# Handing out the side work of a two-layer hybrid encoder by its estimated ScalarE and VectorE time instead of by fixed rates

## The chip, the cores and the metric

The kernel runs on one core of one Trainium2 chip. The metric is the device time of one execution in microseconds, as a median of several runs; the profile shows one execution, with a span from its first to its last instruction.

## The reference

The input is a sequence of 512 tokens of 1024 channels in float32. Two layers run one after the other, each with three residual blocks behind an RMSNorm:

```
h = h + 1/2 * SwiGLU_1(RMSNorm(h))        # 1024 -> 2816 -> 1024
h = h + Mixer(RMSNorm(h))
h = h + 1/2 * SwiGLU_2(RMSNorm(h))
```

The mixer has one input projection of 7168 columns that feeds three branches, and all of them are projected, gated by sigmoids of the input, summed and projected once more:

- a Hyena branch: two long convolutions of 512 channels over time, with gates between them, whose filters come from a small sine network (in the kernel: transforms by matmul, called "filter" for the spectra of the filters and "hyena" for the convolutions);
- dilated sliding-window attention in three groups of eight heads, with a position bias (in the kernel: "bias" writes rows of the bias to DRAM, "attn0" and "attn1" each do four heads of all three groups);
- a gated linear recurrence forward and backward over time (in the kernel "rg").

After the second layer comes a last RMSNorm.

## The kernel before

Every large projection is computed with weights and activations split into two parts of reduced mantissa (float32r), as three matmuls: hi by hi, lo by hi, hi by lo. The work is a list, `prog`, of **main steps**. A step loads a block of weights (`load`, L220: 512 rows by 256 columns, 512 KB, two buffers `raw`), splits it (`prep`: a copy on ScalarE into `whi`, L238, and a subtraction on VectorE into `wlo`, L239; twice 128x512 a step, five buffers each), and then issues 24 matmuls of 512 columns (`pair` and `mm3`, L166 to L168). `load` and `prep` run up to three steps ahead. Two such steps make a pair of outputs, which is evacuated from PSUM by `evac` on ScalarE and VectorE; the pool for these outputs has three buffers.

The **side work** (filter, bias, vecs, rg, hyena, attn and some small ones) is written as generators: each piece up to a `yield` is one side step, with its own small matmuls, ScalarE and VectorE instructions and DMAs. `push` puts a generator on one of two lanes, `pump(n)` runs n side steps and takes turns between the lanes, and `drain(name)` runs the rest of a generator at once, because what follows in the list needs its result (or its buffers). The program is traced in this order, and each engine works through its instructions in an order that the scheduler of the framework makes from it: earlier in the trace goes first where both are ready.

The rate decides how many side steps follow a main step:

```
                credit[0] += rate[0]
                pump(int(credit[0]))
                credit[0] -= int(credit[0])
```

The rate is 1 in general, RF = 1.35 from the push of "filter" to its drain, and RM = 1.6 from the push of "rg" to the end of the mixer. These rates count steps, whatever is in them.

Main steps of a mixer, numbered from 1, as the prediction uses them: 1 to 8 the input of rg (after which `push("rg")` follows); 9 to 26 `quad(0)`, the values, queries and keys of four heads (25 and 26 the last keys, evacuated by `together`, L1221), then `push("attn0")`; 27 to 30, 31 to 34 and 35 to 38 the three inputs of Hyena (`conv_in`; after the first of them `push("hyena")`); 39 to 50 `gateproj(2)`, four times two steps of gate (tile `gt`) and one of projection (tile `pj`), with `drain("rg")` after step 40; then `drain("attn0")`; 51 to 68 `quad(1)`, then `push("attn1")`; 69 to 80 `gateproj(0)` with `drain("hyena")` after step 70, since the projection of step 71 reads what Hyena made; 81 to 92 `gateproj(1)` with `drain("attn1")` after step 82; 93 to 100 the output projection.

One half of one order of "hyena" (there are four of them) has these side steps: two transposes with a split (zt), two transforms (xf: twelve matmuls of 256 columns each, L790 to L793 behind them), one of six VectorE operations (zm, zp; L799 to L804), two of four (L809 to L815), one of six (ua to wb; L819 to L826), an empty one, and two that transform back (yc: eight matmuls, then L841, L842, and in the second order the split into yah and yal that `pj` reads). The first of "bias" are three empty steps, and then 24 that each copy one small tile (`row`, L574) and write it 16 times to DRAM (L575).

Of the kernel before, what the change touches and what calls it, by code (L numbers as in the profile page):

```python
# [19 lines left out]
F32R = mybir.dt.float32r  # L20
# [11 lines left out]
NS = 35  # L32
HP = 20
F0, F1 = 0, 6
RF, RM = 1.35, 1.6
TWO_PI = 2.0 * math.pi


def shape_constants():
# [65 lines left out]
    ("hy_skip", 8), ("rg_conv_w", 16), ("rg_conv_b", 4),  # L105
    ("rg_ba", 8), ("rg_bx", 8), ("rg_lambda", 8), ("b_gate", 24),
]


@with_exitstack  # L110
def trunk(ctx: ExitStack, tc: tile.TileContext, A, out, depth=DEPTH):
    nc = tc.nc
# [17 lines left out]
    def slot(name, dt=F32):  # L130
        return sp.tile([128, 2, 512], dt, tag="sl", name=name)

    def tmp(name, dt=F32):
        return tp.tile([128, 512], dt, tag="t", name=name)
# [10 lines left out]
    def flat(t):  # L145
        return t.rearrange("p a b -> p (a b)")

    def split(hi, lo, src):
        S.copy(hi, src)
        V.tensor_tensor(lo, src, hi.bitcast(F32), ALU.subtract)  # L150
# [28 lines left out]
    def main(fn, src=None, kc=4, cols=256):  # L179
        prog.append((fn, src, kc, cols, 0))  # L180

    def pump(n, lane=None):
        for _ in range(n):
            live = [q for q in lanes if q]
            if lane is not None:
                live = [q for q in live if q is lane]
            while live:
                q = live[turn[0] % len(live)]
                turn[0] += 1
                try:  # L190
                    next(q[0][1])
                    break
                except StopIteration:
                    alive.discard(q[0][0])
                    q.popleft()
                    live = [x for x in live if x]
            else:
                return

    def push(name, gen, lane=0):  # L200
        alive.add(name)
        lanes[lane].append((name, gen))

    def drain(name):
        while name in alive:
            pump(1, next(q for q in lanes if any(n == name for n, _ in q)))

    rate, credit = [1], [0]
    first = [True]

    def run_prog():
        wsteps = [i for i, p in enumerate(prog) if p[1] is not None]
        raws, made = {}, {}
        nxt_raw, nxt_prep = [0], [0]

        def load(j):
            _, src, kc, cols, _ = prog[wsteps[j]]
            raw = rp.tile([128, 4, 256], F32, tag="raw", name="raw")
            if cols == 256:
                nc.sync.dma_start(raw[:, :kc], src.rearrange("(k p) n -> p k n", p=128))  # L220
            else:
                for k in range(kc):
                    dst, rows = raw[:, 2 * k:2 * k + 2], slice(128 * k, 128 * k + 128)
                    nc.sync.dma_start(dst, src[rows].rearrange("p (g c) -> p g c", c=256)
                                      if len(src.shape) == 2 else src[rows])
            raws[j] = raw

        def prep(j, half=None):
            _, src, kc, cols, _ = prog[wsteps[j]]
            if cols == 512:  # L230
                kc *= 2
            raw = raws[j]
            parts = made.setdefault(j, [])
            for k0 in range(0, kc, 2) if half is None else (2 * half,):
                kk = min(2, kc - k0)
                hi = wp.tile([128, 2, 256], F32R, tag="hi", name="whi")
                lo = wp.tile([128, 2, 256], F32R, tag="lo", name="wlo")
                S.copy(hi[:, :kk], raw[:, k0:k0 + kk])  # L238
                V.tensor_tensor(lo[:, :kk], raw[:, k0:k0 + kk], hi.bitcast(F32)[:, :kk], ALU.subtract)  # L239
                if cols == 512:  # L240
                    parts.append((flat(hi), flat(lo)))
                    continue
                for k in range(kk):
                    parts.append((hi[:, k], lo[:, k]))
            if half in (None, 1):
                del raws[j]

        def ahead(n):
            while nxt_raw[0] < min(n, len(wsteps)):
                load(nxt_raw[0])  # L250
                nxt_raw[0] += 1

        def prepare(n):
            while nxt_prep[0] < min(n, len(wsteps)):
                prep(nxt_prep[0])
                nxt_prep[0] += 1

        norm = state["norm"]
        load_x(0)
        ahead(1)  # L260
        load_x(1)
        norm.squares(0)
        norm.half(0, lambda i: i in (1, 2) and prep(0, i - 1))
        nxt_prep[0] = 1
        ahead(2)
        norm.copies()
        norm.half(1)
        prepare(2)
        norm.copies()
        norm.squares(1)  # L270
        norm.end()
        j = 0
        for i, (fn, src, kc, cols, _) in enumerate(prog):
            if src is None:
                fn()
            else:
                with tc.high_priority(HP):
                    ahead(j + 3)
                    prepare(j + 3)
                fn(made.pop(j))  # L280
                j += 1
                credit[0] += rate[0]
                pump(int(credit[0]))
                credit[0] -= int(credit[0])
        pump(10 ** 6)

    def pair(W, X, evac, name):
# [151 lines left out]
    def h(k):  # L439
        return hs[k // 2][:, k % 2]  # L440
# [9 lines left out]
    def load_x(a):  # L450
        if a == 0:
            rows_to_cols(g0, A["ffn1_norm"][0], 8)
        for b in range(4):
            nc.sync.dma_start(xt[b][:, a], A["x"][b::4, a * 512:a * 512 + 512])
# [41 lines left out]
    hyst = [dict() for _ in range(depth)]  # L496

    def ffn(l, which, next_norm):
        wg, wu, wd = A[f"ffn{which}_wg"][l], A[f"ffn{which}_wu"][l], A[f"ffn{which}_wd"][l]
        hid = []  # L500
        X = lambda: state["norm"].x
        for fp in range(DFF // 256):
            st = {}

            def ev_g(c, ps, st=st):
                t = tmp("silu")
                V.tensor_tensor(t, ps, state["norm"].R, ALU.mult)  # L507
                S.activation(t, t, AF.Silu)
                st[c] = t

            def ev_u(c, ps, st=st):
                if c == 0:
                    st["hi"], st["lo"] = slot("hidh", F32R), slot("hidl", F32R)
                t = tmp("up")
                V.tensor_tensor(t, ps, state["norm"].R, ALU.mult)  # L515
                V.tensor_tensor(t, t, st[c], ALU.mult)
                split(st["hi"][:, c], st["lo"][:, c], t)
                hid.append((st["hi"][:, c], st["lo"][:, c]))

            pair(wg[:, fp * 256:(fp + 1) * 256], X, ev_g, "g")  # L520
            pair(wu[:, fp * 256:(fp + 1) * 256], X, ev_u, "u")
            if which == 1 and fp == F0:
                main(lambda: (push("filter", hy_filter(l, hyst[l])), rate.__setitem__(0, RF)))
            if which == 1 and fp == F1:
                main(lambda: (drain("filter"), rate.__setitem__(0, 1)))
                if l == 0:
                    main(lambda: (push("bias", bias_rows()), push("vecs", load_vectors(range(1, depth), 4))))

        def begin():
            state["next"] = next_norm()  # L530

        if next_norm is None:
            down_tokens(wd, hid)
            return
        main(begin)
        for d in range(4):
            def ev_d(c, ps, d=d):
                k = 2 * d + c
                V.scalar_tensor_tensor(h(k), ps, 0.5, h(k), ALU.mult, ALU.add)
                state["next"].add(k, h(k))  # L540

            pair(wd[:, d * 256:(d + 1) * 256], lambda: hid, ev_d, "d")

        def end():
            hid.clear()
            state["next"].end()
            state["norm"] = state["next"]

        main(end)
# [589 lines left out]
    def mixer(l, next_norm):  # L1139
# [50 lines left out]
                pair(W[:, c0 + o + i * 256:c0 + o + i * 256 + 256], X, ev, key)  # L1190
        main(lambda: drain("xn"))
        main(lambda: push("rg", rg(l, srg)))
        main(lambda: rate.__setitem__(0, RM))

        def apart(st, g, c, ps):

# [162 lines left out]
        def end():  # L1359
            state["next"].end()  # L1360
            state["norm"] = state["next"]
            del state["mx"]
            rate[0] = 1

        main(end)


# [81 lines left out]
    for l in range(depth):  # L1449
# [6 lines left out]
        else:  # L1456
            main(lambda: push("ht", to_tokens()))
            ffn(l, 2, None)
    run_prog()


# [33 lines left out]
```

## Time and profile before

| | us |
|---|---|
| median of three runs | 2874.32 |
| lowest and highest of them | 2872.74, 2874.44 |
| the profiled execution | 2872.54 |
| its span | 2870.8 |
| TensorE busy in the span | 2838.4 |
| VectorE busy | 1693.0 |
| ScalarE busy | 1220.3 |
| mean granted clock of TensorE | 0.996 |

The profiled execution lasts 1.74 us longer than its span and 1.78 us less than the median of the runs. Matmuls overlap in the records, so that a busy TensorE can still run below its full pace; the number of matmuls in a stretch shows that better than the busy time.

### The profile page before, as it was taken

The page shows a single profiled execution, that of the slowest core. Times are in us where ns is not written, and L with a number is a line of the kernel's source. Part 1 is how long each engine was busy: PE and PEld are TensorE (multiplying, and loading weights), DVE is VectorE, ACT ScalarE, POOL GpSimd, SP SyncE. Part 2 cuts the span into 40 slices and gives each one's busy share as a digit, 9 for nine tenths or more (in the row PEclk, how much of TensorE's full clock was granted, in tenths as well). Part 3 has the DMA queues.
Part 4 walks back from the last instruction along what each step waited for, and adds up shares of the span by engine and source line. Part 5 has one row for each costly group of instructions (what it writes and reads, how often), then busy time and mean ns, then how long its engine had stood idle before and what let it go on. Part 6 is the DMA issues. An engine that isn't in the chain of part 4 may idle for free.

```text
span 2870.8 us, 35848 instructions
## 1 busy us (share of the span) xinstructions
PE 2838.4 (99%) x13379; PEld 2360.9 (82%) x13379; DVE 1693.0 (59%) x3076; ACT 1220.3 (43%) x2133; POOL 172.5 (6%) x321
## 2 busy tenths in 40 slices
PE   9999999999999999999999999999999999999998
PEld 7887888778888888888888888887888888888887
DVE  5784447586776555444377743566757755654533
ACT  5442335845333543333244432377443353433323
POOL 2011110010001000000010000001100110000000
PEclk9999999999999999999999999999999999999999
DMA  4436633242233233332334333333322322333332
GB/s 139 129 112 130 137 118 103 83 121 94 81 96 92 67 125 96 98 101 93 99 110 137 114 96 114 114 98 102 106 88 88 101 80 74 125 96 96 96 103 96
DMA packets 260735, 297.54 MB, mean 104 GB/s; under 512 B 14196, under 2 KB 241632, under 8 KB 260560
## 3 DMA queue, kind: packets, MB, share of 16 engines
q1 hardware_dynamic: 244240, 256.41, 29.1%
q0 software_dynamic: 16160, 38.77, 5.6%
q8 instruction: 105, 1.72, 0.2%
q14 instruction: 70, 0.57, 0.1%
q10 hardware_dynamic: 160, 0.07, 0.0%
HBM read 276.84 MB, written 18.35 MB: 103 GB/s over the span
## 4 chain that ended last, share of the span: by engine, by line
PE 91%; ACT 4%; DVE 2%; DMA 1%; issue 1%; ACTq 0%; DVEq 0%
PE g L166 6%; PE g L167 6%; PE g L168 6%; PE u L166 5%; PE u L167 5%; PE u L168 5%; PE d L168 4%; PE d L167 4%; PE d L166 4%; PE gt L166 3%; PE gt L168 3%; PE gt L167 3%; PE pj L167 1%; PE pj L168 1%; PE pj L166 1%; PE y L1435 1%
## 5 line engine op out<-in xcount | busy, mean ns | idle before, releaser
L239 DVE TENSOR_TENSOR wlo<-raw,whi 128x512 fp32r<-128x512 f32 x928 | 635.9, 689 | 784.8 <-ACT whi L238 773.1
L238 ACT CAST whi<-raw 128x512 fp32r<-128x512 f32 x928 | 572.8, 620 | 1074.6 <-PE u L167 232.1
L166 PE MATMUL g<-xh,whi 128*128 128x512 f32 x696 | 273.3, 393 | 2.8 <-DVE up L515 2.8
L166 PE MATMUL u<-xh,whi 128*128 128x512 f32 x704 | 275.2, 391 | 0.0
L167 PE MATMUL u<-xl,whi 128*128 128x512 f32 x704 | 274.7, 390 | 0.0
L168 PE MATMUL u<-xh,wlo 128*128 128x512 f32 x704 | 274.6, 390 | 0.0
L167 PE MATMUL g<-xl,whi 128*128 128x512 f32 x696 | 272.2, 391 | 0.0
L168 PE MATMUL g<-xh,wlo 128*128 128x512 f32 x696 | 272.2, 391 | 0.0
L166 PE MATMUL d<-hidh,whi 128*128 128x512 f32 x528 | 205.9, 390 | 0.0
L168 PE MATMUL d<-hidh,wlo 128*128 128x512 f32 x528 | 205.8, 390 | 0.0
L167 PE MATMUL d<-hidl,whi 128*128 128x512 f32 x528 | 205.7, 390 | 0.0
L166 PEld LDWEIGHTS g<-xh,whi 128*128 128x128 f32 x696 | 131.3, 189 | 30.7 <-DVE up L515 3.9
L168 PEld LDWEIGHTS u<-xh,wlo 128*128 128x128 f32 x704 | 132.3, 188 | 27.3
L166 PEld LDWEIGHTS u<-xh,whi 128*128 128x128 f32 x704 | 132.3, 188 | 27.2 <-DVE silu L507 0.5
L167 PEld LDWEIGHTS u<-xl,whi 128*128 128x128 f32 x704 | 132.4, 188 | 26.6
L168 PEld LDWEIGHTS g<-xh,wlo 128*128 128x128 f32 x696 | 131.2, 188 | 26.9
L167 PEld LDWEIGHTS g<-xl,whi 128*128 128x128 f32 x696 | 131.3, 189 | 26.5
L166 PE MATMUL gt<-nh,whi 128*128 128x512 f32 x384 | 152.8, 398 | 0.3 <-DVE mrg L1292 0.3
L167 PE MATMUL gt<-nl,whi 128*128 128x512 f32 x384 | 150.0, 391 | 0.0
L168 PE MATMUL gt<-nh,wlo 128*128 128x512 f32 x384 | 150.0, 391 | 0.0
L167 PEld LDWEIGHTS d<-hidl,whi 128*128 128x128 f32 x528 | 99.2, 188 | 20.6
L166 PEld LDWEIGHTS d<-hidh,whi 128*128 128x128 f32 x528 | 99.2, 188 | 20.5
(467 smaller groups left out, 5579.3 us busy)
## 6 DMA issues: line engine op xcount, KB each, us to landing
raw<-in_w_in SPq DMA_DIRECT2D x96, 512.0 KB, 3.5
raw<-in_ffn_wg SPq DMA_DIRECT2D x88, 512.0 KB, 3.7
raw<-in_ffn_wu SPq DMA_DIRECT2D x88, 512.0 KB, 3.8
raw<-in_ffn_wd SPq DMA_DIRECT2D x60, 512.0 KB, 3.5
raw<-in_w_gate SPq DMA_DIRECT2D x48, 512.0 KB, 3.6
raw<-in_ffn_wd SPq DMA_DIRECT2D x56, 256.0 KB, 2.7
raw<-in_w_in SPq DMA_DIRECT2D x32, 256.0 KB, 3.0
raw<-in_w_out SPq DMA_DIRECT2D x16, 512.0 KB, 3.4
```

What stands on the lines that cost most here:

```text
L166: T.matmul(ps, lh, rh, start=first, stop=False)
L167: T.matmul(ps, lh, rl, start=False, stop=False)
L168: T.matmul(ps, ll, rh, start=False, stop=last)
L238: S.copy(hi[:, :kk], raw[:, k0:k0 + kk])
L239: V.tensor_tensor(lo[:, :kk], raw[:, k0:k0 + kk], hi.bitcast(F32)[:, :kk], ALU.subtract)
L1435: T.matmul(ps, xh[:, tok], wh, start=(k == 0), stop=False)
```

## The change

The two rates go. After each main step `pace` sums, by a formula for each instruction that was traced since the last look, the time that ScalarE, VectorE and TensorE would take (`estimate`): 0.2 us and 0.85 ns an element of the free dimension for ScalarE, 0.15 us and 1.05 ns for VectorE (6.5 ns for a reciprocal), 0.013 us and 0.417 ns a column for a float32r matmul, and 1.7 ns a column for another. What ScalarE or VectorE have over TensorE is kept as `owed`, never below zero. Then up to LANE = 2 side steps run, and none is begun while the larger of the two debts, with the side steps just taken, is above AHEAD = 3.0 us. Drains stay as they were, and what they issue is counted at the next look. The computation is the same, instruction for instruction; what changes is where in the trace the side steps stand. The matmuls of the undilated scores (`score0`) take rounded float32r parts in both kernels: the diff doesn't touch them.

```diff
--- before.py
+++ after.py
@@ -32,7 +32,7 @@
 NS = 35
 HP = 20
 F0, F1 = 0, 6
-RF, RM = 1.35, 1.6
+AHEAD, LANE = 3.0, 2
 TWO_PI = 2.0 * math.pi
 
 
@@ -107,6 +107,20 @@
 ]
 
 
+def estimate(i):
+
+    if not i.outs:
+        return None, 0.0
+    n = math.prod(c for _, c in i.outs[0].ap[1:])
+    if i.engine == mybir.EngineType.Activation:
+        return 0, 0.2 + 0.85e-3 * n
+    if i.engine == mybir.EngineType.DVE:
+        return 1, {"InstReciprocal": 6.5e-3, "InstTensorTensorScan": 2.4e-3}.get(type(i).__name__, 1.05e-3) * n + 0.15
+    if i.engine == mybir.EngineType.PE:
+        return 2, 0.013 + 0.417e-3 * n if i.ins[1].dtype == F32R else 1.7e-3 * n
+    return None, 0.0
+
+
 @with_exitstack
 def trunk(ctx: ExitStack, tc: tile.TileContext, A, out, depth=DEPTH):
     nc = tc.nc
@@ -205,7 +219,27 @@
         while name in alive:
             pump(1, next(q for q in lanes if any(n == name for n, _ in q)))
 
-    rate, credit = [1], [0]
+    owed, given, seen = [0.0, 0.0], [0.0, 0.0, 0.0], [0]
+
+    def count():
+        todo = nc.cur_bb.bb.instructions
+        for i in todo[seen[0]:]:
+            e, t = estimate(i)
+            if e is not None:
+                given[e] += t
+        seen[0] = len(todo)
+
+    def pace():
+
+        count()
+        for e in range(2):
+            owed[e] = max(owed[e] + given[e] - given[2], 0.0)
+        given[:] = 0.0, 0.0, 0.0
+        for _ in range(LANE):
+            if max(owed[e] + given[e] for e in range(2)) > AHEAD:
+                break
+            pump(1)
+            count()
     first = [True]
 
     def run_prog():
@@ -279,9 +313,7 @@
                     prepare(j + 3)
                 fn(made.pop(j))
                 j += 1
-                credit[0] += rate[0]
-                pump(int(credit[0]))
-                credit[0] -= int(credit[0])
+                pace()
         pump(10 ** 6)
 
     def pair(W, X, evac, name):
@@ -520,9 +552,9 @@
             pair(wg[:, fp * 256:(fp + 1) * 256], X, ev_g, "g")
             pair(wu[:, fp * 256:(fp + 1) * 256], X, ev_u, "u")
             if which == 1 and fp == F0:
-                main(lambda: (push("filter", hy_filter(l, hyst[l])), rate.__setitem__(0, RF)))
+                main(lambda: push("filter", hy_filter(l, hyst[l])))
             if which == 1 and fp == F1:
-                main(lambda: (drain("filter"), rate.__setitem__(0, 1)))
+                main(lambda: drain("filter"))
                 if l == 0:
                     main(lambda: (push("bias", bias_rows()), push("vecs", load_vectors(range(1, depth), 4))))
 
@@ -1190,7 +1222,6 @@
                 pair(W[:, c0 + o + i * 256:c0 + o + i * 256 + 256], X, ev, key)
         main(lambda: drain("xn"))
         main(lambda: push("rg", rg(l, srg)))
-        main(lambda: rate.__setitem__(0, RM))
 
         def apart(st, g, c, ps):
 
@@ -1360,7 +1391,6 @@
             state["next"].end()
             state["norm"] = state["next"]
             del state["mx"]
-            rate[0] = 1
 
         main(end)
```

## Rows read from the trace of the kernel before

**Rows 1.** The page: span, then busy us, share, instructions of each engine.

```profile
span 2870.8 us, 35848 instructions
PE 2838.4 (99%) x13379; PEld 2360.9 (82%) x13379; DVE 1693.0 (59%) x3076; ACT 1220.3 (43%) x2133; POOL 172.5 (6%) x321
```

**Rows 2.** Who TensorE waited for: us in total, times, longest.

```profile
PE v L166 <- ACT k L1221: 11.3, 2, 5.9
PE g L166 <- DVE up L515: 2.8, 1, 2.8
```

**Rows 3.** Windows in SwiGLU: busy us (instructions) by engine, clock, DMA share, GB/s.

```profile
1296.00:1368.00 72.00, 72.00 (x320) 59.65 (x319) 30.08 (x45) 22.41 (x37) 0.00 (x0) 1.00 0.29 94
```

**Rows 4.** Windows, around the three stalls and around the end of attn1.

```profile
570.00:582.00 12.00, 6.64 (x23) 5.00 (x21) 11.62 (x14) 7.32 (x11) 3.69 (x7) 0.73 0.27 71
1986.00:2004.00 18.00, 12.11 (x43) 9.49 (x42) 16.32 (x21) 10.20 (x13) 4.71 (x9) 0.81 0.21 53
270.00:282.00 12.00, 9.23 (x34) 6.81 (x33) 8.43 (x16) 4.14 (x7) 1.78 (x3) 0.86 0.55 59
966.00:990.00 24.00, 23.06 (x134) 19.67 (x134) 15.60 (x16) 8.47 (x14) 0.00 (x0) 1.00 0.10 29
...
576.00:582.00 6.00, 3.58 (x9) 2.83 (x9) 5.62 (x7) 3.46 (x5) 2.59 (x5) 0.50 0.23 55
```

**Rows 5.** Groups of ScalarE, 540 to 580 us: busy us, mean ns, idle before.

```profile
L943 ACT ACTIVATE ti<-psg,vec 64x512 f32<-64x512 f32 x8 | 5.5, 683 | 0.2
...
L238 ACT CAST whi<-raw 128x512 fp32r<-128x512 f32 x9 | 5.4, 609 | 1.4 <-DMA raw<-in_w_in 1.3
L944 ACT ACTIVATE aa<-tr,rgs 128x512 f32<-128x512 f32 x4 | 3.3, 816 | 0.1
...
L946 ACT ACTIVATE qq<-aa 128x512 f32<-128x512 f32 x4 | 2.5, 618 | 0.0
```

**Rows 6.** Timeline of ScalarE ahead of the first long stall: start, us, instruction, idle.

```profile
541.25 1.28 ACT L942 ACT_TABLE_LOAD   x1
542.55 0.68 ACT L942 ACTIVATE tr<-psg,vec 64x512 f32<-64x512 f32 x1
...
575.75 2.13 ACT L149 CAST ych<-gx 128x512 fp32r<-128x512 f32 x2 [2.08 <-DVE gx L967]
577.78 1.06 ACT L1221 COPY k<-k 128x512 f32<-128x512 f32 x2
```

**Rows 7.** DMA queues, 222 to 276 us: packets, MB, share of 16 engines' stretch.

```profile
q0 software_dynamic: 869, 1.48, 38.6%
q1 hardware_dynamic: 4939, 4.89, 27.4%
...
dbias<-row POOLq DMA_DIRECT2D x8, 192.0 KB, 8.8
```

**Rows 8.** Who ScalarE waited for, 222 to 276 us.

```profile
ACT whi L238 <- DMA raw<-in_ffn_wu: 14.2, 3, 6.3
```

**Rows 9.** Tiles xf, yc, pj near 870 us: durations ns, first to last start.

```profile
L168 PE MATMUL xf<-zh,ftl x8: 279/282/284, 842.5 to 850.6; 128*128 128x256 f32 x8
...
L836 PE MATMUL yc<-invt,wa x8: 271/274/276, 872.6 to 880.8; 128*128 128x128 f32 x8
...
L166 PE MATMUL pj<-yah,whi x8: 388/390/477, 881.5 to 886.5; 128*128 128x512 f32 x8
```

**Rows 10.** Groups of VectorE, 849 to 885 us: busy us, mean ns, idle before.

```profile
L239 DVE TENSOR_TENSOR wlo<-raw,whi 128x512 fp32r<-128x512 f32 x12 | 8.2, 689 | 6.3 <-ACT whi L238 6.3
...
L819 DVE TENSOR_TENSOR ua<-yy 128x1024 f32<-128x1024 f32 x1 | 1.2, 1227 | 0.0
...
L824 DVE TENSOR_TENSOR wa<-ua 128x512 f32<-128x512 f32 x1 | 0.7, 687 | 0.0
...
L802 DVE TENSOR_TENSOR zp<-x,x 128x256 f32<-128x256 f32 x1 | 0.4, 420 | 0.0
```

**Rows 11.** Groups of TensorE, 966 to 992 us.

```profile
L166 PE MATMUL gt<-nh,whi 128*128 128x512 f32 x13 | 5.1, 390 | 0.0
```

## The prediction

> **What bounds the kernel now.** I read the page first: TensorE is busy for 2838.4 of 2870.8 us, VectorE and ScalarE for 1693.0 and 1220.3 [rows 1]. Where nothing disturbs it TensorE does 320 matmuls in 72 us, 0.225 us each [rows 3], so a main step of 24 lasts 5.4 us. The change issues no instruction less or more; it can only move the stretches in which TensorE falls behind that pace. The list of what TensorE waited for names two of weight: 11.3 us, in two pieces, before the first matmul of a pair v, for a copy k of ScalarE, and 2.8 us for VectorE's `up` [rows 2]. The windows around them show the whole loss, since the clock drops as well [rows 4]. From 570 to 582 us there are 23 matmuls where 53 fit: 30 x 0.225 = 6.8 us lost, with a granted clock of 0.50 in the second half (the lower of its two levels, 1.2 of 2.4 GHz). From 1986 to 2004 there are 43 for 80: 8.3 us. From 270 to 282 there are 34 for 53: 4.3 us. Together 19.4 us, 0.7%: this is what better spreading could win at most, but for small change.
>
> **Why those stalls are there.** The first two lie at main step 27 of each mixer, behind the densest part of rg. One gate step of rg has four tanh of 0.68, two of 0.81 and one of 0.62 on ScalarE, 5.0 us, and a main step beside it 2 x 0.61 of splits and some 0.6 to 1.2 of evacuation (an estimate: two or four instructions a pair like L238's) [rows 5]; it has 4 matmuls of its own, so TensorE needs 5.4 + 0.9 = 6.3 us while ScalarE needs 6.8 to 7.4. At a rate of 1.6, every second or third main step takes two. A table load of 1.28 us comes on top, and just before the stall two casts `ych` stand ahead of the copies of k in ScalarE's order, which wait 2.1 us for VectorE [rows 6]. The third is a different thing: the bias rows. From 222 to 276 us eight row writes of 192 KB take 38.6% of the 16 DMA engines, the weights 27.4% [rows 7], and ScalarE waits three times, 14.2 us in all, for weights to land [rows 8].
>
> **The new order, walked through the code.** The formula prices a main step at 24 x 0.2265 = 5.44 us of TensorE, and its two splits at 1.27 (ScalarE) and 1.38 (VectorE). I added the evacuation of each pair and the price of each side step by the same formula and went through the mixer step by step, from step 9 on, where the debt is nought. The results are positions, not times. (1) rg: a gate step is priced at 4.45 us of ScalarE, so they go one to a main step, at 17 to 20 and 23 to 25 and 27, with none at 26, where before two stood at 16 and at 23. rg ends at main step 35 instead of 29, before its drain at 40. (2) hyena starts at 37 instead of 32, never gets more than two steps, and is stopped whenever one of its VectorE steps (3.1 to 5.2 us by the formula) leaves more than 3.0 of debt. Its last pair xf stands behind step 69 instead of 65. At the drain behind step 70 six filled steps are left, 17.0 us of VectorE; before, none were. (3) That lump leaves 15 us of debt, so attn1 gets nothing for four main steps, and its drain behind step 82 holds 11 filled steps (14.7 ScalarE, 15.9 VectorE, 19.6 TensorE) instead of 6 (7.6, 8.3, 10.9). attn0's drain grows from 5 to 8. (4) filter: 6 instead of 12 steps are left at its drain in the first layer. (5) bias: its steps cost the formula next to nothing, so they go two to a main step: 27 in 15 main steps instead of in 27. A VectorE price 5% lower would leave hyena 3 filled steps, with 3.9 us of VectorE; the walk is that sensitive.
>
> **What each costs.** *rg, spread.* ScalarE then needs 6.8 to 7.4 us a main step against 6.3, a debt of under 1 us a step that step 26 pays back (1.8 against 5.4). I take both stalls as gone, -6.8 - 8.3 = -15.1. The bound on the other side is 0: the formula knows no table load, no 0.81 us tanh, and no wait for VectorE, so the copies can still be late.
>
> By the Trainium skill ("ScalarE: Activation LUTs", section on what ACT_TABLE_LOAD costs) a change of tables takes 1283 ns and a drain of 1380 ns behind it. In this trace the load lasts 1.28 us and the next activation starts 0.02 us after it [rows 6], so no drain is seen; by the page each load would leave 1.4 us more of unpriced work, and the gain of 15.1 would shrink by that much for each load ahead of the copies.
>
> *hyena, late.* This is the largest cost. Behind the last xf comes a chain that only VectorE can do: two additions (1.4 us), zm and zp (2 x 0.69 + 4 x 0.42), the products (4 x 1.22 + 4 x 0.69), ua to wb (2 x 1.22 + 4 x 0.69) [rows 10], 17.3 us by the records, some 15.5 as they overlap by about 0.08 each; at least three splits of weights get in between, 2.0. Then eight yc matmuls and the last two rounds of three VectorE operations and a cast, about 6.4. So from the last xf to the last part that `pj` reads it is 24 us. Before, the last xf began at 850.6, yc at 872.6 and `pj` at 881.5 us [rows 9], 31 us later: that was covered. Four main steps later, TensorE has in these 24 us only main step 70 (5.4), 32 yc matmuls of 0.11 (3.5), the six `pj` matmuls whose inputs are there (1.4), and what the order can pull forward. How much that is, the end of attn1 shows: 39 gt matmuls where the pair's second half has 24 [rows 11], 15 x 0.225 = 3.4 us, and some 1.5 of attn1's scores. That leaves 24 - 15.2 = 9 us idle. I take 7, as the earlier halves of the result come some 2 us sooner, and 2 for the clock behind it (0.73, 0.81 and 0.86 over the three windows of a stall [rows 4]): 9 a layer, 18 in all. Bounds: 0, if hyena is 4 main steps further than I count; 26, if nothing can be pulled forward.
>
> *attn1 and attn0.* At the end of attn1 TensorE now loses 0.9 us of 24 [rows 4]. A longer lump brings its own TensorE work (19.6 against 14.7 and 15.9), so I add 1 a layer, bounds 0 and 5. Nothing in TensorE's list waits for attn0 at its drain; 0, covered by `quad(1)`, and 1 a layer without that cover.
>
> *bias, twice as dense.* A row write costs 0.386 x 54 / 8 = 2.6 us of all 16 engines and a weight block 0.274 x 54 / 9.3 = 1.6 [rows 7]. Two rows and one block per main step are 6.8 against 5.4 us, for four main steps: 5.5 us short, of which the blocks loaded ahead cover about one step. The later rows, of 128 KB, just fit. I expect 6 lost where 4.3 are lost now [rows 4], +2, bounds -4 and +8.
>
> By the Trainium skill ("DMA: Bandwidth & Descriptors", section "Issuing engines are not separate DMA queues") transfers from several issuers share the same 16 engines and interleave. The late weights [rows 8] agree; it speaks against handing out steps by ScalarE and VectorE time alone.
>
> *filter.* Its drain is halved in the first layer: -1, bounds -2 and 0; TensorE loses little there now.
>
> **Sum.** -15.1 + 18 + 2 + 2 - 1 = +6 on the profiled 2872.5, that is 2878.5, say 2879. The profile lies inside the runs' spread, 1.8 below their median 2874.3, so this is +0.16% on the median: no change, or slightly slower. About 0.2% is what a measurement here can tell from no change.
>
> **The rivals.**
> *The spread wins* (other side): hyena is 3 or more main steps further than I count, or the scheduler covers its chain. For it: a VectorE price 5% off is enough. Against it: attn0 and hyena share the two steps per main step. It decides from a last xf at main step 66 or earlier on. -15.1 + 2 + 2 - 1: 2861.
> *ScalarE is still late*: the debt the formula doesn't see keeps the stall at step 27, and hyena stalls as well. For it: before, the same walk gives a debt of 6.5 us at its highest, two steps ahead of the stall, and 2.5 when it comes; the rest the formula doesn't see. Against it: the walk's debt now ends at nought there. 2879 + 15 = 2893.
> *Row writes starve TensorE*: 10 us instead of 6, through DMA alone; 2885 or so with the rest as forecast. The section of the Trainium skill's page on DMA named above would lead there.
> *The brake never acts*, the count finds nothing, and two steps follow every main step: rg's 10 us of ScalarE stand against 7.2, the two stalls at least double, hyena is early. 2872.5 + 15: 2888.
>
> **How the numbers follow.** Forecast 0.48 (own range 2868 to 2891), the spread wins 0.28, ScalarE late 0.12, row writes 0.07, no brake 0.05. Faster than 2868.6: 0.05 of the forecast's share and 0.26 of the second: 0.31. Slower than 2880: 0.23, 0.11, 0.05 and 0.05: 0.44. The same: the rest, 0.25. The range cuts the lower part of the second case and the upper part of the third: 2857 to 2894.
>
> **What will show it.** Right: no wait of v for k, ScalarE below 5.9 of 6 us in rg's second half; 17 us of VectorE work without a gap after the last xf, and `pj` waiting for yah or yal, with a low clock behind it, in both layers; row writes all issued within about 75 us. Wrong: the last xf 20 us or more ahead of the first yc, as now; or the v stall still there; or `pj` not among what TensorE waits for, which would give the second case.

## The result and the profile after

The kernel after takes 2914.82 us (median of 4 runs, 2910.16 to 2916.59) against 2874.38 for the kernel before: a ratio of 1.0139, 95% interval 1.0122 to 1.0157. It is 40.4 us slower, far above the range of the prediction. The profiled execution lasts 2916.59 us.

Line numbers behind `estimate` are higher by 14, behind `pace` by 34, and behind the place that calls it by 32 or 31: `whi` is L272, `wlo` L273, `silu` L539, `up` L547, the row copy L606, the row write L607, the matmuls L180 to L182.

The page of the kernel after, its first two rows, beside [rows 1]:

```profile
span 2914.8 us, 35858 instructions
PE 2853.6 (98%) x13379; PEld 2364.9 (81%) x13379; DVE 1691.2 (58%) x3076; ACT 1221.7 (42%) x2133; POOL 172.7 (6%) x321
```

The work is the same and the span is 44.0 us longer. To see where, I took from both traces the start of every 240th matmul on split weights (the same ten main steps lie between two of them in both) and subtracted; some of these rows, in us:

```
main steps begun   before    after    difference
 20                 131.9     137.3      +5.4
 30                 202.2     209.1      +6.9
 40                 264.8     286.1     +21.3
 50                 324.5     358.3     +33.9
 80                 490.6     524.9     +34.3
100                 629.5     652.6     +23.1
160                1048.4    1083.8     +35.4
230                1430.1    1465.5     +35.5
280                1732.6    1772.9     +40.3
330                2034.6    2067.1     +32.5
390                2455.5    2499.5     +44.0
460                2840.9    2884.9     +44.0
```

Inside a stretch the difference also moves because side matmuls stand elsewhere (of the 6.9 at step 30 most is such: in e1 below, where 7.6 stand there, 0.4 are left at step 40); between stretches it is a loss. Up to step 80 the first layer has lost 34 us, its mixer then adds 1.1, the filter of the second layer 4.8 and the second mixer 3.7. So nearly all of it is lost between 210 and 360 us, where the rows of the bias are written.

Who TensorE waited for in the kernel after (us in total, times, longest), the rows that answer to [rows 2]:

```profile
PE u L180 <- DVE silu L539: 15.8, 2, 8.1
PE g L180 <- DVE up L547: 5.8, 2, 5.2
PE psg L972 <- DVE rgwl L164: 3.9, 2, 1.9
PE g L180 <- DVE v L1354: 3.8, 2, 1.9
PE yc L868 <- DVE wa L855: 2.9, 2, 1.5
```

The wait of v for a copy k is gone. In its place stand two small ones in rg's stretch, 1.9 us a layer each (`psg` for a split, `g` for the short convolution of `v`), and the two long ones of 15.8 and 5.8 for `silu` and `up` of the SwiGLU. Windows of the kernel after over the bias rows, to be read against [rows 3] (columns as there):

```profile
216.00:288.00 72.00, 56.58 (x224) 43.73 (x223) 27.13 (x52) 15.54 (x26) 8.31 (x14) 0.90 0.65 100
288.00:360.00 72.00, 60.92 (x243) 48.63 (x242) 27.09 (x48) 17.50 (x30) 12.24 (x23) 0.89 0.64 101
```

224 and 243 matmuls stand where an undisturbed stretch has 320: (96 + 77) x 0.225 = 39 us lost, some 4 of which the kernel before loses too. VectorE and ScalarE are *less* busy than usual. The DMA queues from 215 to 345 us, against [rows 7]:

```profile
q0 software_dynamic: 2560, 3.76, 46.6%
q1 hardware_dynamic: 8335, 8.27, 19.4%
...
raw<-in_ffn_wg SPq DMA_DIRECT2D x4, 512.0 KB, 12.2
dbias<-row POOLq DMA_DIRECT2D x16, 128.0 KB, 9.0
dbias<-row POOLq DMA_DIRECT2D x8, 192.0 KB, 9.4
```

The row writes take 46.6% of the 16 engines, the weights 19.4%; a block of wg lands after 12.2 us (median over the whole run: 3.6). Two stalls in the order of ScalarE and of VectorE (start, us, instruction, idle before it):

```profile
251.63 0.62 ACT L272 CAST whi<-raw 128x512 fp32r<-128x512 f32 x1 [9.65 <-DMA raw<-in_ffn_wu]
...
274.27 0.62 ACT L272 CAST whi<-raw 128x512 fp32r<-128x512 f32 x1 [12.26 <-DMA raw<-in_ffn_wg]
```

```profile
285.82 0.88 DVE L606 COPY row<-mk 8x256 f32<-8x256 f32 x4
293.15 0.69 DVE L547 TENSOR_TENSOR up<-u,R 128x512 f32<-128x512 f32 x1 [6.45 <-DMA dbias<-row]
```

Twice ScalarE, with VectorE behind it, waits for weights; behind 285.82 four row copies have taken four of the six `tmp` buffers, and `up` waits 6.45 us until a write has landed and frees one. So there are two paths from a slow write to TensorE: late weights, and held buffers.

The late end of hyena, tiles of the kernel after (first layer, durations in ns, first to last start), against [rows 9]:

```profile
L182 PE MATMUL xf<-zh,ftl x8: 279/282/283, 894.8 to 903.0; 128*128 128x256 f32 x8
```
```profile
L868 PE MATMUL yc<-invt,wa x8: 275/275/377, 920.2 to 923.6; 128*128 128x128 f32 x8
```

The last xf stands behind main step 69 (69.0 by the count of matmuls since the first of rx; 65.0 before), as walked, and the last yc ends 21 us later. TensorE's groups in between:

```profile
L180 PE MATMUL gt<-nh,whi 128*128 128x512 f32 x17 | 6.7, 395 | 0.0
...
L868 PE MATMUL yc<-invt,wa 128*128 128x128 f32 x8 | 1.6, 288 | 1.5 <-DVE wa L855 1.5
```

It loses only 1.5 us ahead of yc, since 51 matmuls of gt (17 of each of three kinds) stand there, 27 of them pulled forward.

### The profile page after: what moved, and what is told of

It is laid out like the page before. It is cut to its first block, busy times and chain, and to the rows that moved or that the text cites. A ratio compares the mean times of both kernels' runs of the same rounds, so it can differ in the third digit from the quotient of the medians.

```text
span 2914.8 us, 35858 instructions
## 1 busy us (share of the span) xinstructions
PE 2853.6 (98%) x13379; PEld 2364.9 (81%) x13379; DVE 1691.2 (58%) x3076; ACT 1221.7 (42%) x2133; POOL 172.7 (6%) x321
## 4 chain that ended last, share of the span: by engine, by line
PE 83%; DVE 6%; issue 5%; ACT 4%; DMA 1%; POOL 1%; ACTq 0%; DVEq 0%; POOLq 0%
PE g L180 5%; PE g L181 5%; PE g L182 5%; PE u L180 5%; PE u L181 5%; PE u L182 5%; PE d L181 4%; PE d L180 4%; PE d L182 4%; PE gt L182 3%; PE gt L180 3%; PE gt L181 3%; PE pj L181 1%; PE k L180 1%; PE pj L182 1%
## 5 line engine op out<-in xcount | busy, mean ns | idle before, releaser
L273 DVE TENSOR_TENSOR wlo<-raw,whi 128x512 fp32r<-128x512 f32 x928 | 636.3, 689 | 805.7 <-ACT whi L272 796.4
L272 ACT CAST whi<-raw 128x512 fp32r<-128x512 f32 x928 | 573.0, 620 | 1061.2 <-PE u L181 235.6
L180 PE MATMUL u<-xh,whi 128*128 128x512 f32 x704 | 276.8, 393 | 15.8 <-DVE silu L539 15.8
L180 PE MATMUL g<-xh,whi 128*128 128x512 f32 x696 | 274.0, 394 | 7.8 <-DVE up L547 5.8
L182 PE MATMUL u<-xh,wlo 128*128 128x512 f32 x704 | 275.7, 392 | 0.0
L182 PE MATMUL g<-xh,wlo 128*128 128x512 f32 x696 | 272.9, 392 | 0.0
L180 PE MATMUL d<-hidh,whi 128*128 128x512 f32 x528 | 206.3, 391 | 2.8 <-DVE up L547 2.2
L182 PE MATMUL d<-hidh,wlo 128*128 128x512 f32 x528 | 206.1, 390 | 0.0
L180 PEld LDWEIGHTS u<-xh,whi 128*128 128x128 f32 x704 | 133.4, 189 | 44.3 <-DVE silu L539 17.1
L180 PEld LDWEIGHTS g<-xh,whi 128*128 128x128 f32 x696 | 131.8, 189 | 36.8 <-DVE up L547 6.7
L182 PEld LDWEIGHTS u<-xh,wlo 128*128 128x128 f32 x704 | 133.2, 189 | 27.8
L182 PEld LDWEIGHTS g<-xh,wlo 128*128 128x128 f32 x696 | 131.6, 189 | 27.4
L180 PE MATMUL gt<-nh,whi 128*128 128x512 f32 x384 | 152.2, 396 | 1.6 <-ACT gz L1315 1.6
L182 PE MATMUL gt<-nh,wlo 128*128 128x512 f32 x384 | 149.9, 390 | 0.0
L180 PEld LDWEIGHTS d<-hidh,whi 128*128 128x128 f32 x528 | 99.4, 188 | 24.3 <-DVE up L547 2.7
L182 PEld LDWEIGHTS d<-hidh,wlo 128*128 128x128 f32 x528 | 99.6, 189 | 20.7
```

The lines of the kernel that those rows point to most:

```text
L180: T.matmul(ps, lh, rh, start=first, stop=False)
L182: T.matmul(ps, ll, rh, start=False, stop=last)
```

## The experiments

All times are medians, and ratios and differences stand against the kernel before on the same chip, unless another kernel is named; the medians of the kernel before on these chips lie within 0.8 us of each other. Rows of a run name the lines of its own kernel. The theory at the start: handing out two row steps a main step costs some 30 us. The main rivals: lumps in the mixer; and, for how it costs, held buffers against full DMA engines.

**One row step a main step** (`e1_bias_one`, on the kernel after):

```diff
-        for _ in range(LANE):
+        for _ in range(1 if "bias" in alive else LANE):
```

> The kernel after, but while the bias rows are being written only one side step follows a main step (as before the change). Theory 'dense rows' (the 33 us that the kernel after falls behind between main steps 30 and 50 of the first layer come from handing out two row steps a main step): 2915 - 30 = 2885 us, 2881 to 2889. Rival 'lumps in the mixer' (hyena and attn1 end late, as the prediction had it, and the row stretch only shows the loss first): within 3 us of 2915.

Measured: 2883.64 us, ratio 1.0034 (1.0021 to 1.0047), 31.2 less than after. The density of the rows is the cause of most of the loss.

**The kernel before with two** (`e3_before_two`):

```diff
-                credit[0] += rate[0]
+                credit[0] += 2 if "bias" in alive else rate[0]
```

> The kernel before, with its fixed rates, but two side steps follow a main step while the bias rows are being written. Theory 'dense rows': 2874 + 30 = 2904 us, 2898 to 2910, all of it between 215 and 345 us. Rival 'lumps in the mixer': within 3 us of 2874.

Measured: 2910.78 us, ratio 1.0128 (1.0111 to 1.0145), 37.2 more than before and 0.8 above the range that I gave. This one edit of the kernel before gives 9 tenths of the whole result. All of it lies in that stretch (main steps 30 to 50; the difference stays at 35.4 up to step 90).

**Rows without copies** (`e2_no_row`, on the kernel after; the bytes written are the same):

```diff
-                row = tmp("row")[0:8, 0:w]
-                V.tensor_copy(row, mk[0:8, cs])
-                nc.gpsimd.dma_start(wide[:, r0:r0 + 16], row.unsqueeze(1).to_broadcast([8, 16, w]))
+                nc.gpsimd.dma_start(wide[:, r0:r0 + 16], mk[0:8, cs].unsqueeze(1).to_broadcast([8, 16, w]))
```

> The kernel after, with two row steps a main step as it is, but the row copy is left out: the 24 writes read the masked bias itself, so that no write holds one of the six buffers that silu and up of the SwiGLU need, and VectorE has no copy that waits for such a buffer. The bytes written are the same. Theory 'held buffers' (VectorE stands in order behind row copies that wait for earlier writes to land): the loss goes, 2885 us, 2880 to 2891. Rival 'full DMA engines' (the writes themselves delay the weights): nothing is won, 2908 to 2918, and ScalarE still waits 40 us or more for raw weights between 215 and 345 us. Half and half would be about 2900.

Measured: 2916.69 us, ratio 1.0149 (1.0134 to 1.0164): nothing won. The test is not quite clean. The copies had also paced the writes; without them GpSimd issues all eight of a group within 5 us (first at 223.9, last at 228.1). But it shows that no held buffer is needed for the loss. Waits of that kernel from 215 to 345 us, and its DMA queues from 224 to 258:

```profile
ACT whi L272 <- DMA raw<-in_ffn_wg: 45.9, 3, 26.5
...
PE g L180 <- ACT whi L272: 15.0, 1, 15.0
```
```profile
q0 software_dynamic: 896, 1.58, 83.2%
q1 hardware_dynamic: 935, 0.93, 7.8%
...
raw<-in_ffn_wg SPq DMA_DIRECT2D x2, 512.0 KB, 29.1
```

These 34 us are worth reading closely, in the trace's records of single packets. That both queues have about the same number of them, 896 and 935, means little. Of those of the row queue only 384 carry rows: 320 of 4608 bytes, 1.37 us each (median), and 64 of 1536 bytes, 0.41 us; the other 512 hold 12 or 4 bytes and took 0.009 us. A packet of weights holds 1 KB and took 0.046 us. The two blocks of wg, 512 such packets each, were issued at 227.1 and 232.6. None of them started before 234, 428 by 256, and 473 in the next 2 us, when the rows were all but through. The blocks landed at 258.3 and 259.7, with the last of the eight writes (258.1). So while many rows are being written, weights hardly come through. By what rule an engine chooses between the two queues the records don't show: they don't name the engine.

**Rows in buffers of their own** (`e5_own`, on the kernel after):

```diff
+        own = [slot("rows") for _ in range(4)]
...
-                row = tmp("row")[0:8, 0:w]
+                row = own[r0 // 32][0:8, r0 // 16 % 2, 0:w]
```

> The kernel after, two row steps a main step, each row copy kept in its place on VectorE, but the copies go to eight buffers of their own, so that no write holds a buffer of silu and up. Unlike the run without copies, the writes then can't be issued ahead of VectorE's order. Theory 'held buffers': 2885 us, 2880 to 2891. Theory 'slow writes' (eight writes of 192 KB and two blocks took 34 us in the run without copies, some 3.9 us a write, so that two writes and a block need 9.4 us where a main step has 5.4): as slow as after, 2906 to 2918, with whi waiting for raw weights 40 us or more between 215 and 345 us.

Measured: 2895.65 us, ratio 1.0077 (1.0062 to 1.0092), between the two forecasts. The trace says why. The first eight copies, now free, all ran from 223.2 to 226.7 us, their writes left together, and TensorE stood still for 13.9 us on a block of wg that ScalarE awaited for 25.4. The other 16 writes left between 266 and 370 us, mostly one a main step. Its wait for wg from 215 to 345 us, and its windows:

```profile
ACT whi L272 <- DMA raw<-in_ffn_wg: 31.8, 3, 25.4
```
```profile
216.00:288.00 72.00, 58.15 (x244) 45.87 (x243) 29.88 (x55) 16.18 (x28) 7.31 (x12) 0.91 0.71 103
288.00:360.00 72.00, 72.00 (x319) 59.63 (x318) 28.72 (x50) 21.10 (x36) 5.97 (x10) 1.00 0.50 127
```

Bunched, the writes cost the whole loss of the first window; one at a time they cost nothing in the second, with DMA still at 0.50 (there all are of 128 KB, and the bunched ones of 192). The packet records show a reason. One write alone has 8 or 9 packets in flight: that of 281.1 moved its 32 packets of 4096 bytes in 3.0 us, 0.67 us each (median), and the writes of this run that were alone took 1.8 to 3.7 us, with a median of 2.9. In e2, eight writes of this size at once have up to 17 in flight from 268.5 to 290.9 us, of 1.17 us each: 2.8 us a write. So a second write beside the first moves hardly any more rows; it doubles the packets in flight, and each takes longer. As it is, this edit changed the spacing again, and held buffers and spacing can't be parted by it. That `up` waits on held buffers is in the trace of after; how much it alone costs stays open.

**Rows on 128 partitions** (`e6_wide`, on the kernel after; 24 writes of the same sizes, six shared buffers, two a main step; the rows lie in DRAM in another order and are read back from it):

```diff
...
-            nc.gpsimd.dma_start(mk[0:8, cs], A[f"mask{g}"])
+            nc.gpsimd.dma_start(mk[:, cs], A[f"mask{g}"][0:1].to_broadcast([128, BW[g]]))
...
-            T.matmul(ps[0:8, 0:w], rel[:, g * 8:g * 8 + 8], oh[0:N_BUCKETS, cs], start=True, stop=True)
+            many = oh[0:N_BUCKETS, 896:1024]
+            V.tensor_copy(many.rearrange("p (r h) -> p r h", h=8),
+                          rel[:, g * 8:g * 8 + 8].unsqueeze(1).to_broadcast([N_BUCKETS, 16, 8]))
+            T.matmul(ps[:, 0:w], many, oh[0:N_BUCKETS, cs], start=True, stop=True)
...
-                nc.gpsimd.dma_start(wide[:, r0:r0 + 16], row.unsqueeze(1).to_broadcast([8, 16, w]))
+                nc.gpsimd.dma_start(wide[8 * r0:8 * r0 + 128], row)
...
```

> The kernel after, two row steps a main step and the six shared buffers as they are, but the rows lie on 128 partitions (16 copies of the 8 heads, made by the same matmul with 16 times as many columns of weights), and each of the 24 writes sends 128 rows from 128 partitions instead of 8 rows 16 times. Same bytes, same number of writes; the bias is read back from another layout. Theory 'slow writes' (it is the 8 partitions and few DMA engines a write that make it dear, not its bytes): a write lands in 4 us or less instead of 9, the loss of the stretch goes wholly, 2880 us, 2876 to 2885. Rival 'bytes' (the writes are dear for their 3.6 MB): 2910 to 2918. If the buffers were what counts and the writes only release them sooner, 2880 as well: the run before tells that apart.

Measured: 2879.32 us, ratio 1.0017 (1.0007 to 1.0027), 35.5 less than after. DMA queues from 215 to 345 us:

```profile
q0 software_dynamic: 1664, 3.75, 8.3%
...
dbias<-row POOLq DMA_DIRECT2D x16, 128.0 KB, 2.1
dbias<-row POOLq DMA_DIRECT2D x8, 192.0 KB, 2.4
```
```profile
216.00:288.00 72.00, 72.00 (x313) 58.03 (x312) 40.40 (x79) 22.79 (x38) 13.17 (x24) 1.00 0.46 145
```

The same bytes in 8.3% of the engines instead of 46.6%, each write landed after 2.1 to 2.4 us instead of 9.0 to 9.4, and the stall is gone at full density. It was not the bytes: it was how the writes were laid out. By itself this run doesn't tell full engines from held buffers, which come free sooner too; e2 does.

**The kernel before with wide rows** (`e9_before_wide`, the edit of e6 on before):

> The kernel before, fixed rates, with the rows on 128 partitions as in the run on wide rows. Theory 'slow writes': the third stall of the kernel before, 4.3 us between 270 and 282, and nothing else goes: 2874 - 5 = 2869 us, 2867 to 2871. Rival 'the rows hurt only when two go to a main step': within 1.5 us of 2874.

Measured: 2868.37 us, ratio 0.9980 (0.9971 to 0.9990), 5.5 less. The third stall of [rows 4] was of the same kind; the two waits of v stay at 11.3 us.

**Debts in the mixers alone** (`e4_mixer_only`, the kernel after with the old rates restored outside):

```diff
...
+        if rate[0]:
+            owed[:], given[:] = (0.0, 0.0), (0.0, 0.0, 0.0)
+            credit[0] += rate[0]
+            pump(int(credit[0]))
+            credit[0] -= int(credit[0])
+            return
...
```

> The kernel after in the mixers only: from the push of rg to the end of the mixer side steps are handed out by the debts, everywhere else by the old fixed rates (1, and 1.35 for the filter). Theory from the positions of main steps in the two traces (the mixers of the two layers grew by 1.1 and 3.7 us, the spread of rg wins about 11 us a layer and the later steps give it back): 2874 + 5 = 2879 us, 2876 to 2882. Rival 'the mixer wins what the stalls of rg cost, and is only disturbed by what comes before it': 2874 - 15 = 2859 us, 2857 to 2864.

Measured: 2877.75 us, ratio 1.0014 (1.0005 to 1.0024): +4.2. The mixers by themselves lose a little. Against e1, which differs in the pacing of the filter and of what little else lies outside the mixers, it is 5.9 faster: that is what debts cost there. By the starts of main steps 3.2 us of it arose in the second layer's filter (against before, from step 230 to 280, e1 goes from 2.4 to 6.6 us and e4 from -0.2 to 0.8) and 1.0 ahead of the first mixer. Waits of TensorE in the kernel after from 1440 to 1700 us, where the kernel before has none:

```profile
PE mlp L661 <- ACT hywr L656: 1.6, 1, 1.6
PE hps L712 <- ACT wo L701: 0.7, 1, 0.7
PE mlp L662 <- DVE hywr L657: 0.5, 1, 0.5
```

The two waits for hywr are 2.1 us of it: two steps in one main step put a small matmul right behind the split that it reads.

**A larger debt behind rg** (`e8_debt8`, on e4):

```diff
-            if max(owed[e] + given[e] for e in range(2)) > AHEAD:
+            if max(owed[e] + given[e] for e in range(2)) > (AHEAD if "rg" in alive else 8.0):
```

> The kernel with debts in the mixers only (2877.8), but once rg is done a side step is begun up to a debt of 8.0 us instead of 3.0. Theory 'late hyena' (hyena, stopped by its own VectorE steps, and the attn1 lump behind it give back what the spread of rg wins): hyena ends earlier and 2 to 4 us a layer come back: 2872 us, 2868 to 2875. Rival 'the losses are elsewhere' (the first wait of v behind rg, the products of rg): within 1.5 us of 2878. Rival 'the brake is right': two steps a main step starve the evacuation instead, 2880 to 2890.

Measured: 2865.92 us, ratio 0.9972 (0.9962 to 0.9983), 11.8 less than e4 and more than I expected. The last xf now stands behind main step 64 instead of 69, and from 835 to 1040 us TensorE waits for one thing only; in e4 it waits there for 3.9 us:

```profile
PE pj L182 <- DVE ybl L165: 0.4, 1, 0.4
```
```profile
PE yc L877 <- DVE wa L864: 1.5, 1, 1.5
PE pj L181 <- ACT ybh L164: 0.9, 2, 0.5
PE gt L181 <- ACT gz L1325: 0.8, 1, 0.8
PE pj L181 <- ACT yah L164: 0.5, 1, 0.5
```

The brake of 3.0 us, not the spread of rg, was what the mixers lost by.

**Both** (`e10_both`, e8 with the rows of e6), **no brake behind rg** (`e11_no_brake`, e10 with 100.0 in place of 8.0) and **a tighter brake in rg** (`e12_rg15`, e10 with 1.5 in place of AHEAD):

> The kernel with debts in the mixers only, up to 8.0 us once rg is done (2865.9), with the rows on 128 partitions. If the two causes are apart their gains add: 2866 - 5 = 2861 us, 2858 to 2864. If the gain of the wide rows were one of timing in the first layer's mixer: 2864 to 2868.

> As the kernel with both, but once rg is done two side steps follow every main step, whatever the debt (limit 100 us). Theory 'late hyena' carried on: the earlier the better, 2857 to 2861 us. Rival 'the brake is needed': steps of 5 us go two at a time, the evacuation of pairs is late on VectorE, 2863 to 2875.

> As the kernel with both, but while rg is alive no side step is begun above a debt of 1.5 us instead of 3.0. The traces of all kernels with debts show two new waits in rg's stretch, 2.1 us before psg for a split of VectorE and 2.1 us before g for a copy of VectorE, in each layer. Theory 'lumps': with smaller debts these shrink, 2855 to 2859 us. Rival 'later': rg and with it hyena end later, the gain is lost again, 2861 to 2868.

Measured: 2859.94 us for both, ratio 0.9952 (0.9937 to 0.9967), faster than either kernel; the gains of e9 and e8 add (5.5 + 8.1 = 13.6, and 13.9 found). Without the brake 2860.65 (0.9954, 0.9940 to 0.9969): a limit of 8.0 or none makes no difference that can be measured, and the rival 'the brake is needed' falls; nor did it help that hyena came earlier still (last xf behind step 63 instead of 64). With 1.5 in rg 2865.83 (0.9971, 0.9960 to 0.9982): the rival 'later' holds. The two waits of 1.9 a layer go, but rg's last `psg` moves from main step 27 to 36, the last xf from 64 to 67, and other waits come:

```profile
PE g L181 <- DVE g L1367: 3.0, 2, 1.5
PE pj L181 <- ACT ych L164: 2.7, 6, 0.7
```

## Why the prediction was wrong, point by point

| term | forecast, us | measured, us | from |
|---|---|---|---|
| rg, spread | -15.1 | about -8 | e8 against before: all that debts do in the mixers with the limit of 8.0, put down to rg |
| hyena late, attn1 and attn0 | +18 + 2 | about +12 | e4 against e8 |
| the mixers together | +4.9 | +4.2 | e4 against before |
| bias, twice as dense | +2 (-4 to +8) | +30 to +37 | e6 less e9: 35.5 - 5.5; after against e1: 31.2; e3 against before: 37.2 |
| filter | -1 | +5.9 | e1 against e4 |

30 + 5.9 + 4.2 = 40.1 of the 40.4 us measured. (With the 31.2 of e1 in place of 30 the terms are differences in a row, which must add up.)

**The step that failed** is "*bias, twice as dense*": +2, and never over +8. Its mechanism, two writes and a block needing more DMA time than a main step has, is the right one, and the rival "row writes starve TensorE" names it; the size was wrong in both. Three things in it were off.

First, the price. 2.6 us a write was the share of all engines over 54 us in which the writes were spread [rows 7]. In a row they cost 0.832 x 34 / 8 = 3.5 us. By that two writes and a block are 8.6 us against 5.4. Nor do the later rows, of 128 KB, "just fit": eight of them took from 268.5 to 290.9 us in e2, 2.8 us each, and of the matmuls that the kernel after lacks, 77 (17 us) lack in the window from 288 us on, where only such rows are written.

Second, I let the block pay its own 1.6 us and no more. The landing times stood in the trace: 8.8 us for a write [rows 7], ScalarE waiting up to 6.3 us for weights [rows 8]. I counted 14.2 us in all; the same list has 8.1 more, for wg:

```profile
ACT whi L238 <- DMA raw<-in_ffn_wg: 8.1, 2, 7.1
```

In e2 two blocks that came upon a burst of eight writes were held for nearly as long as it lasted, 31.2 and 27.0 us. A kernel that loads two or three steps ahead is stalled by that for much more than the sum of the shares; how much for shorter bursts, no run measures apart.

Third, the spacing. I took 27 steps in 15 main steps, 75 us, as if evenly. The rows were copied from 222.9 to 333.3 us. The count was right, as the 24 writes lie within 13 main steps of TensorE; the longer time is the stall itself. But they left in bursts of up to four, since the copies stand in VectorE's order behind work that is itself late. What the bursts cost beyond the density is not shown.

The Trainium skill ("DMA: Bandwidth & Descriptors", section "Rules for kernel authors") says that an outermost dimension of c < 16 confines a transfer to at most c engines. The rows have 8 heads outermost. The traces agree as far as they go: in e2 the writes land in pairs, at 232.8 and 233.9, 241.9 and 242.7, 250.5 and 251.7, as if two shared the engines, and a write alone has 8 or 9 packets in flight where two or more have 16 or 17. But the number of engines can't be the whole price, since more writes at once, with twice the packets in flight, moved rows no faster (2.8 us for 128 KB against a median of 2.9). e6 changes the partitions and the outermost dimension together, so no run here shows which of the two counts.

**rg.** Both waits of v went, as forecast. That gave less than 15.1, since a wait of 1.9 us before `psg` and one before `g` came instead in each layer: `psg` reads what VectorE has yet to split, and `g` waits for the convolution of `v` on VectorE. With smaller debts in rg (e12) both go. I also counted one table load ahead of the old stall; from 540 to 580 us the trace has three, of 1.28 us each.

**hyena.** The walk was exact: last xf behind step 69, not 65. The chain behind it took about the 24 us that were added up. What was mis-sized is the cover: I counted 15 of gt pulled forward and there were 27 (51 against the 24 of the pair's second half), 2.7 us more, and the granted clock stayed at 1.00: 1.5 us was waited at yc instead of 7. `pj` waited for yah as forecast, but for 0.5 us. More of the 12 us lies at the end of attn1 than the 1 a layer that I gave it. There TensorE of the kernel after waits, from 990 to 1035 us, for the following, and at the same place in e8 for `ybl` alone:

```profile
PE pj L180 <- ACT ybh L163: 0.9, 2, 0.6
PE gt L180 <- ACT gz L1315: 0.8, 1, 0.8
```

By the waits the two ends share about evenly: from 835 to 1040 us e4 waits 2.0 us before `yc` and for `yah`, 1.9 for `ybh`, `gz` and `pt`, and e8 0.4 in all. In both layers the waits make up 6.6 of the 12 us; what the rest is stays open.

**filter.** I took the shorter drain for a small gain; nothing was lost there, and the denser start made new waits.

**The other rivals.** ScalarE was not late, and the brake acted: e8 and e11 show that it acted too much. "The spread wins" has its condition (last xf at step 66 or earlier) met in e8: 2866 us, where it forecast 2861.

Two errors of opposite sign cancelled in the mixers, so that their sum of +5 was right for no good reason. Of the miss of 36 us the rows are some 29, the filter 7.

## What to carry to other kernels

A budget that prices two engines hands out for nothing whatever costs a third: before steps are regrouped by such a formula, list what each issues to the DMA queues, and price it in a burst, not as a mean share. When a transfer takes long for its bytes, look at its layout first: the same 3.6 MB from 128 partitions instead of 8 made the density harmless and also won 5.5 us in the kernel before. And a brake on side work can cost more than it saves where a chain behind it has a due time: a limit of 8.0 instead of 3.0, by which hyena's last xf came five main steps earlier, was worth 12 us.

## What the runs showed of the hardware

Three things that I had not expected. A write of 192 KB from 8 partitions took 8.8 to 9.4 us to land (median), and the same bytes from 128 partitions 2.4; of 128 KB 9.0 and 2.1 (in e5, with no other write beside it, 4.6: issued at 310.1, landed at 314.7). Several such writes at once moved rows no faster than one alone: in e2 16 or 17 packets of 4096 bytes in flight took 1.17 us each, in e5 8 or 9 took 0.67, and a write of 128 KB came to 2.8 us and, alone, to a median of 2.9. And the long packets of one queue held up the short ones of the other: beside row packets of 1.37 us, 428 of 1024 weight packets of 0.046 us had started 23 us after the second block was issued, the row queue had 83.2% of the engines' time, and the two 512 KB blocks landed after 31.2 and 27.0 us, where the median of the kernel after is 3.6.
